# A projection whose gates run ahead of its products, on one core: order, sums and mixing moved

## The chip, the cores and the metric

One Trainium2 chip, one of its cores. The metric is the device time of one execution of the whole program in microseconds (us). TensorE (PE) multiplies matrices into PSUM banks; VectorE (DVE), ScalarE (ACT) and GpSimd (POOL) work on tiles of 128 partitions in SBUF; transfers are issued by the queue of SyncE (SP) and by ACT. Each engine runs its own instructions strictly in the order in which they stand, and waits for the others by semaphores.

## The reference, cut to what matters

Two layers. The first (gMLP and dilated attention) is left out here, since nothing in it changes. The second is RWKV-7 time mixing. Its part that matters:

```python
xx = concatenate([zeros_like(h[:, :1]), h[:, :-1]], axis=1) - h
xr, xw, xk, xv, xa, xg = [h + xx * mu[i] for i in range(6)]
r = xr @ w_r
k = xk @ w_k
v = xv @ w_v
g = xg @ w_g
logw = -softplus(-(w0 + tanh(xw @ w1) @ w2)) - 0.5
decay = exp(-exp(logw))
a = sigmoid(a0 + (xa @ a1) @ a2)
kk = hs(k * k_k)
kk = kk * rsqrt(maximum(sum(kk * kk, axis=-1, keepdims=True), 1e-24))
k = k * (1.0 + (a - 1.0) * k_a)
...                                   # rwkv7_scan over r, decay, k, v, kk, a, then the group norm of y
bonus = sum(rh * kh * r_k, axis=-1, keepdims=True) * vh
y = (y + bonus) * silu(g)
return y @ w_o
```

Sequence 1024, width 1024, 16 heads of 64, all float32. Every product of the projections is made of three passes (high by high, high by low, low by high), with each operand split into a rounded part and a rest: `hi` by ACT, `lo = raw - hi` by DVE or POOL.

## The kernel before, in words

The second layer works in this order: the low-rank first factors (`lora`), then three projections r, k and v of four column blocks of 256 (`CB`) each. The list `plan` has the twelve blocks, j = 0 to 3 for r, 4 to 7 for k, 8 to 11 for v. The projections' inputs are mixtures of a token and the one before it: `mixed` makes, for one half `f` of the sequence (512 tokens), eight tiles: `xm` (ACT L736 a scaling, DVE L737 the rest), `xh` (ACT L739) and `xl` (L740, by DVE for odd and by POOL for even tiles). The tiles of r's half f are given back by r's last block only, so k's mixing of half 0 follows r's last product of half 0, and that of half 1 follows r's last product of all; v's mixing stands to k in the same way. After v come the gate's product and the scan over chunks. The gate's mixing of half 1 goes through DRAM (`mixed_out`, L750 to L755): eight units, each with three tiles `xm`, `xh`, `xl` of the ring `s2`, which has seven places, and two stores. Block j = `XD` issues it. The ring `s2` also serves `xm` of `mixed` and `rt`, the tile by which r and v are written out of PSUM (L842, L855).

For r and k a piece is 128 channels (index p) by 512 tokens (half f): 24 matmuls into one of three banks `bA`. There are 16 pieces, and a block of columns has four. In k, `Prep.__call__` takes each finished piece: `ks` is its copy (L789); `pz` holds the gates' two products (two matmuls each, second low-rank factors `rw_w2` and `rw_a2`, loaded and split per piece by `second`, L778 and L779); `tanh` follows (L797); DVE runs a sum along the tokens of each chunk of 64 (L799, L802); ACT exponentiates it both ways (L803, L804); then DVE and POOL build the operands `AR` (L809, L811, L812) and `BK` (L813, L814, L817) of the scan, and `tz` for the bonus (L815, L816 on POOL, L820). Two sums over the channels of each head are made by matmuls with `sel` (L822 of the squares of `ks`, L823 of `tz`), 32 columns of which two are used, into a bank of their own per piece, copied out by L825 and stored. `AR` and `BK` are stored in DRAM (`A_d`, `BK_d`) for the scan.

Up to the scan, the order of the instructions on each engine is chosen when the program is built, by a scheduler of the framework; from the scan on it is written out by hand in tables that the change does not touch.

Of the kernel before, what the change touches and what calls it, by code (L numbers as in the profile page):

```python
# [757 lines left out]
class Prep:  # L758


    def __init__(self, g, a, pool):
# [4 lines left out]

    def second(self, p):

        if p not in self.w2:
# [1 line left out]
            self.w2 = {p: []}
            for n in ("rw_w2", "rw_a2"):
                raw = self.pool.tile([P, P], F32, name="w2", bufs=1)
                for i in range(2):
                    nc.sync.dma_start(raw[64 * i:64 * i + 64], self.a[n][0][:, p * P:(p + 1) * P])
                hi = self.pool.tile([P, P], F32R, name=n + "h", bufs=2)
                lo = self.pool.tile([P, P], F32R, name=n + "l", bufs=2)
                nc.scalar.activation(hi, raw, AF.Copy)  # L778
                nc.vector.tensor_tensor(lo, raw, hi.bitcast(F32), OP.subtract)  # L779
                self.w2[p].append((hi, lo))  # L780
        return self.w2[p]

    def __call__(self, p, f, pk):
        g, nc, pool = self.g, self.g.nc, self.pool
        sl = slice(f * 512, (f + 1) * 512)
# [4 lines left out]
        rt = pool.tile([P, 512], F32, name="rl", bufs=2)  # L790
        nc.sync.dma_start(rt, g.r_d[p][:, sl])
        pz = g.bB([P, 2, 512], "pz")
        tz = pool.tile([P, 2, 512], F32, name="tz", bufs=2)
        for i, ((wh, wl), src, b) in enumerate(zip(self.second(p), (self.TH, self.UA), (g.w0h, g.a0h))):
            nc.tensor.matmul(pz[:, i], wh, src[:, sl], start=True, stop=False)
            nc.tensor.matmul(pz[:, i], wl, src[:, sl], start=False, stop=True)
            nc.scalar.activation(tz[:, i], pz[:, i], AF.Tanh, bias=b[:, p:p + 1], scale=0.5)  # L797
# [1 line left out]
        nc.vector.tensor_scalar(tw, tw, 0.5, 0.5, op0=OP.mult, op1=OP.add)  # L799
# [742 lines left out]
```

## Time and profile before

| | |
|---|---|
| time, median of three runs (lowest, highest) | 1494.33 us (1488.99, 1495.18) |
| the profiled execution: its time, its span | 1504.67 us, 1502.9 us |
| mean granted clock of TensorE | 0.943 |
| busy share of the span: PE, DVE, ACT, POOL | 89%, 62%, 43%, 38% |
| mean transfer rate | 142 GB/s |

The profiled execution took 10.3 us more than the median of the runs, so a sum over its trace is first made in its own times and then set against the median. In the trace, times are from the start of the span; r's products run from 625 to 728 us, those of k from 728 to some 892 us, the last sums of k's pieces at 947 us, and v's last piece is written out at 1005 us.

### The profile page before, as it was taken

The page shows a single profiled execution, that of the slowest core. Times are in us where ns is not written, and L with a number is a line of the kernel's source. Part 1 is how long each engine was busy: PE and PEld are TensorE (multiplying, and loading weights), DVE is VectorE, ACT ScalarE, POOL GpSimd, SP SyncE. Part 2 cuts the span into 40 slices and gives each one's busy share as a digit, 9 for nine tenths or more (in the row PEclk, how much of TensorE's full clock was granted, in tenths as well). Part 3 has the DMA queues.
Part 4 walks back from the last instruction along what each step waited for, and adds up shares of the span by engine and source line. Part 5 has one row for each costly group of instructions (what it writes and reads, how often), then busy time and mean ns, then how long its engine had stood idle before and what let it go on. Part 6 is the DMA issues. An engine that isn't in the chain of part 4 may idle for free.

```text
span 1502.9 us, 28032 instructions
## 1 busy us (share of the span) xinstructions
PE 1330.6 (89%) x11237; PEld 1130.5 (75%) x11237; DVE 933.2 (62%) x1504; ACT 645.2 (43%) x1236; POOL 565.1 (38%) x381
## 2 busy tenths in 40 slices
PE   5899999799989999999998779998878888978877
PEld 5887788688887799878754447996667777768777
DVE  8752536653565337650897898134577778777884
ACT  4422535543553234552654654134444444453322
POOL 9750102130114412211542543024654444477751
PEclk9999999899999999999998989999988999978998
DMA  6386436340523434142385557338486666765412
GB/s 217 85 273 174 126 117 165 80 131 8 168 78 115 139 127 139 36 150 78 88 250 145 121 150 187 78 98 237 110 256 171 163 158 163 204 207 197 153 31 98
DMA packets 256083, 213.19 MB, mean 142 GB/s; under 512 B 80416, under 2 KB 216192, under 8 KB 255952
## 3 DMA queue, kind: packets, MB, share of 16 engines
q1 hardware_dynamic: 232576, 196.11, 45.1%
q10 hardware_dynamic: 23376, 15.27, 3.8%
q8 instruction: 89, 1.46, 0.4%
q14 instruction: 42, 0.34, 0.1%
HBM read 139.90 MB, written 71.43 MB: 141 GB/s over the span
## 4 chain that ended last, share of the span: by engine, by line
PE 50%; DVE 19%; DMA 10%; ACT 7%; issue 7%; POOL 4%; SPq 3%; ACTq 0%; DVEq 0%; POOLq 0%
PE pj L153 33%; DVE tm L1140 2%; PE pt L572 2%; PE pj L1454 2%; PE pj L711 1%; PE pj L942 1%; DMA Nt<-MA 1%; DMA sg_d<-XT 1%; PE py L1274 1%; PE op L580 1%; ACT wh L105 1%; ACT xm L736 1%; DVE xm L737 1%; PE sp L559 1%; PE sp L562 1%
## 5 line engine op out<-in xcount | busy, mean ns | idle before, releaser
L106 POOL TENSOR_TENSOR wl<-wraw,wh 128x1024 fp32r<-128x1024 f32 x38 | 93.7, 2467 | 164.1 <-ACT wh L105 152.3
L106 DVE TENSOR_TENSOR wl<-wraw,wh 128x1024 fp32r<-128x1024 f32 x46 | 72.2, 1574 | 101.2 <-ACT wh L105 53.4
L153 PE MATMUL pj<-hh,wh 128*128 128x512 f32 x320 | 127.3, 398 | 0.0
L153 PE MATMUL pj<-hh,wl 128*128 128x512 f32 x320 | 126.6, 396 | 0.0
L153 PE MATMUL pj<-hl,wh 128*128 128x512 f32 x320 | 126.6, 396 | 0.0
L105 ACT ACTIVATE wh<-wraw 128x1024 fp32r<-128x1024 f32 x84 | 88.1, 1055 | 67.4 <-DMA wraw<-in_w_in_even_dram 23.0
L153 PE MATMUL pj<-xh,wh 128*128 128x512 f32 x256 | 103.4, 406 | 2.5 <-ACT ks L789 2.4
L153 PE MATMUL pj<-xl,wh 128*128 128x512 f32 x256 | 103.1, 403 | 2.6 <-DVE xl L740 2.6
L153 PE MATMUL pj<-xh,wl 128*128 128x512 f32 x256 | 102.7, 401 | 0.3 <-POOL wl L106 0.3
L566 DVE CUSTOM_DVE_ANT_0 sc<-sp,tb 128x128 f32<-128x128 f32 (+3 forms) x64 | 48.2, 754 | 56.7 <-PE sp L562 48.7
L1454 PE MATMUL pj<-wh,yh 128*128 128x256 f32 x256 | 76.0, 297 | 5.6 <-DVE x L1458 4.1
L1454 PE MATMUL pj<-wh,yl 128*128 128x256 f32 x256 | 75.0, 293 | 4.5 <-POOL yl L106 4.5
L737 DVE SCALAR_TENSOR_TENSOR xm<-hT,pr,xm 128x512 f32<-128x512 f32 x56 | 50.0, 935 | 45.2 <-ACT xm L736 44.8
L153 PE MATMUL pj<-wh,hh 128*128 128x256 f32 x256 | 74.8, 295 | 2.8 <-ACT hh L265 2.5
L153 PE MATMUL pj<-wh,hl 128*128 128x256 f32 x256 | 75.1, 294 | 1.2 <-DVE hl L266 1.2
L153 PE MATMUL pj<-wh,yl 128*128 128x256 f32 x256 | 73.7, 288 | 1.9 <-POOL yl L624 1.9
L1454 PE MATMUL pj<-wl,yh 128*128 128x256 f32 x256 | 74.6, 291 | 0.0
L153 PE MATMUL pj<-wl,hh 128*128 128x256 f32 x256 | 74.3, 291 | 0.0
L153 PE MATMUL pj<-wh,yh 128*128 128x256 f32 x256 | 73.2, 286 | 1.1 <-ACT yh L623 1.1
L153 PE MATMUL pj<-wl,yh 128*128 128x256 f32 x256 | 72.8, 284 | 0.0
L153 PE MATMUL pj<-wh,xh 128*128 128x256 f32 x256 | 72.2, 282 | 0.2
L153 PE MATMUL pj<-wl,xh 128*128 128x256 f32 x256 | 72.2, 282 | 0.0
(323 smaller groups left out, 4131.2 us busy)
## 6 DMA issues: line engine op xcount, KB each, us to landing
wraw<-in_w_in_even_dram SPq DMA_DIRECT2D x28, 512.0 KB
tb<-tb SPq DMA_DIRECT2D x16, 512.0 KB
A_d<-AR SPq DMA_DIRECT2D x16, 512.0 KB
wraw<-in_rw_wg_dram SPq DMA_DIRECT2D x16, 512.0 KB
BK<-BK_d SPq DMA_DIRECT2D x16, 512.0 KB
A<-A_d SPq DMA_DIRECT2D x30, 256.0 KB
xt<-in_x_dram SPq DMA_DIRECT2D x8, 512.0 KB
dv<-vt SPq DMA_DIRECT2D x16, 256.0 KB
```

What stands on the lines that cost most here:

```text
L105: nc.scalar.activation(hi, raw, AF.Copy)
L106: sub.tensor_tensor(lo, raw, hi.bitcast(F32), OP.subtract)
L153: nc.tensor.matmul(ps, a(k), b(k), start=(n == 0), stop=(n == 3 * KT - 1))
L559: nc.tensor.matmul(sp[:, c0:c1], qs[:, b * P:(b + 1) * P], kh[:, c0:c1], start=True, stop=False)
L562: nc.tensor.matmul(sp[:, c0:c1], qs[:, b * P:(b + 1) * P], kl[:, c0:c1], start=False, stop=True)
L566: nc.vector.tensor_tensor_reduce(sc[:, :n], sp[:, :n], tb[:, off:off + n], 1.0, BIG, OP.add, OP.min, mn)
L572: nc.tensor.transpose(pt[:, j - j0, :], sc[:, j * P:(j + 1) * P], g.ident)
L580: nc.tensor.matmul(op[:, s0:QW], vt[:, j, :], pth[j // 4][:, j % 4, s0:QW], start=(j == 0), stop=False)
L711: nc.tensor.matmul(ps, x[:, 2 * kk + i, :], y[:, i, o:o + 512], start=(n == 0), stop=(n == 47))
L737: nc.vector.scalar_tensor_tensor(t, hT[kk, f][:, j, 0:512], g.pr[:, i, k:k + 1], t, op0=OP.mult, op1=OP.add)
L1140: nc.vector.tensor_tensor(tv, D[:, :, 0:t, 0:t], Nd[:, :, t, 0:t][:, :, None, :].to_broadcast([P, 4, t, t]), OP.mult)
L1454: nc.tensor.matmul(ps[:, i, :], u[:, k], v[:, k % 4], start=(k == 0 and j == 0), stop=(k == KT - 1 and j == 2))
```

## The change

`Prep.__call__` is split in three. `gates(p, f)` does what does not need the product (load of r's piece, the gates' products, tanh, the running sum, both exponentials, and two new affine steps on ACT, L822 and L824 of the new code, that take over the scaling of the gate from DVE). `operands` does what needs it: POOL now makes `ks` times the inverse decay (L834) into the place of `BK`'s second half, and DVE multiplies this into both halves (L837, L838); the decays `E` have a column of ones ahead of each chunk, so that `AR` is one instruction (L835) instead of two. `sum` makes the sums of the piece before, with the columns of `sel` moved by p, so that all pieces of a half add up in one bank, which is copied out and stored once per half (L862). `project` calls them: for each piece the gates, then the 24 matmuls, then the sum of the piece before. `second` loads and splits the second factors per block of four pieces and takes the raw tile from the ring `s2`. While j is 4 to 7, the order on PE is that of the program text. `XD` is 8, so `mixed_out` is issued in v's first block.

```diff
-XD = 6
+XD = 8
...
-    g.sel = c.tile([P, 32], F32, name="sel")
+    g.sel = c.tile([P, 40], F32, name="sel")
     nc.vector.memset(g.sel, 0.0)
-    nc.vector.memset(g.sel[0:64, 0:1], 1.0)
-    nc.vector.memset(g.sel[64:128, 1:2], 1.0)
+    nc.vector.memset(g.sel[0:64, 7:8], 1.0)
+    nc.vector.memset(g.sel[64:128, 15:16], 1.0)
...
         self.UA = pool.tile([P, S], F32R, name="UA")
...
+        self.E = [pool.tile([P, 8, CH + 1], F32, name=f"E{i}") for i in range(2)]
+        for E in self.E:
+            g.nc.vector.memset(E[:, :, 0:1], 1.0)
+        self.w2, self.sums, self.n = {}, {}, 0
+        self.due = None
+
+    def second(self, c):
+
+        if c not in self.w2 and c < D // CB:
             g, nc = self.g, self.g.nc
...
+            raw = g.s2([P, 2, CB], F32, "w2")
+            for i in range(2):
+                for j, n in enumerate(("rw_w2", "rw_a2")):
+                    nc.sync.dma_start(raw[64 * i:64 * i + 64, j], self.a[n][0][:, c * CB:(c + 1) * CB])
+            hi = self.pool.tile([P, 2, CB], F32R, name="w2h", bufs=2)
+            lo = self.pool.tile([P, 2, CB], F32R, name="w2l", bufs=2)
+            nc.scalar.activation(hi, raw, AF.Copy)
+            nc.vector.tensor_tensor(lo, raw, hi.bitcast(F32), OP.subtract)
+            self.w2[c] = hi, lo
+
+    def project(self, x, w, c, fs=(0, 1)):
+        g = self.g
+        wh, wl = w
+        self.second(c)
+        for f in fs:
+            for m in range(2):
+                t = self.gates(2 * c + m, f)
+                ps = g.bA([P, 512], "pj")
+                mm3(g.nc, ps, lambda k: wh(k, m), lambda k: wl(k, m),
+                    lambda k: x[0][k // 2, f][:, k % 2, 0:512], lambda k: x[1][k // 2, f][:, k % 2, 0:512])
+                self.sum()
+                self.operands(2 * c + m, f, ps, *t)
+            if f == 0:
+                self.second(c + 1)
+
+    def gates(self, p, f):
+
         g, nc, pool = self.g, self.g.nc, self.pool
-        sl = slice(f * 512, (f + 1) * 512)
+        sl, o = slice(f * 512, (f + 1) * 512), slice((p % 2) * P, (p % 2 + 1) * P)
+        wh, wl = self.w2[p // 2]
+        rt = pool.tile([P, 512], F32, name="rl", bufs=2)
+        nc.sync.dma_start(rt, g.r_d[p][:, sl])
+        pz = g.bB([P, 2, 512], "pz")
+        tz = pool.tile([P, 2, 512], F32, name="tz", bufs=2)
+        for i, (src, b) in enumerate(((self.TH, g.w0h), (self.UA, g.a0h))):
+            nc.tensor.matmul(pz[:, i], wh[:, i, o], src[:, sl], start=True, stop=False)
+            nc.tensor.matmul(pz[:, i], wl[:, i, o], src[:, sl], start=False, stop=True)
+            nc.scalar.activation(tz[:, i], pz[:, i], AF.Tanh, bias=b[:, p:p + 1], scale=0.5)
+        tw, ta = tz[:, 0], tz[:, 1]
+        nc.vector.tensor_scalar(tw, tw, 0.5, 0.5, op0=OP.mult, op1=OP.add)
+        nc.vector.tensor_tensor_scan(tw, g.smask.rearrange("p c t -> p (c t)"), tw, 0.0, op0=OP.mult, op1=OP.add)
+        E, self.n = self.E[self.n % 2], self.n + 1
+        nc.scalar.activation(E[:, :, 1:CH + 1], tw.rearrange("p (c t) -> p c t", t=CH), AF.Exp, scale=-C0)
+        nc.scalar.activation(tw, tw, AF.Exp, scale=C0)
+        nc.gpsimd.tensor_copy(g.EC[:, p, f * 8:(f + 1) * 8, None], E[:, :, CH:CH + 1])
+        BK = pool.tile([P, 8, 2, CH], F32, name="BK", bufs=2)
+        nc.scalar.activation(BK[:, :, 0, :], ta.rearrange("p (c t) -> p c t", t=CH), AF.Identity,
+                             bias=g.kkn[:, p:p + 1], scale=g.kkn[:, p:p + 1])
+        nc.scalar.activation(ta, ta, AF.Identity, bias=g.kam[:, p:p + 1], scale=g.kah[:, p:p + 1])
+        return rt, tw, ta, E, BK
+
+    def operands(self, p, f, pk, rt, En, ta, E, BK):
+        g, nc, pool = self.g, self.g.nc, self.pool
         kk, rk = g.pr[:, 8, p:p + 1], g.pr[:, 10, p:p + 1]
         c3 = lambda t: t.rearrange("p (c t) -> p c t", t=CH)
         ks = pool.tile([P, 512], F32, name="ks", bufs=2)
         nc.scalar.activation(ks, pk, AF.Copy)
...
         AR = pool.tile([P, 8, 2, CH], F32, name="AR", bufs=2)
...
+        nc.gpsimd.tensor_tensor(BK[:, :, 1, :], c3(ks), c3(En), OP.mult)
+        nc.vector.scalar_tensor_tensor(AR[:, :, 0, :], c3(ks), kk, E[:, :, 0:CH], op0=OP.mult, op1=OP.mult)
+        (nc.vector if p % 2 else nc.gpsimd).tensor_tensor(AR[:, :, 1, :], c3(rt), E[:, :, 1:CH + 1], OP.mult)
+        nc.vector.tensor_tensor(BK[:, :, 0, :], BK[:, :, 0, :], BK[:, :, 1, :], OP.mult)
+        nc.vector.tensor_tensor(BK[:, :, 1, :], c3(ta), BK[:, :, 1, :], OP.mult)
         nc.gpsimd.tensor_tensor(ta, ta, ks, OP.mult)
-        nc.vector.tensor_tensor(BK[:, :, 1, :], c3(ta), En, OP.mult)
-        sq = ks
-        nc.scalar.activation(sq, ks, AF.Square, scale=kk)
         nc.vector.scalar_tensor_tensor(ta, rt, rk, ta, op0=OP.mult, op1=OP.mult)
...
+        nc.scalar.activation(ks, ks, AF.Square, scale=kk)
+        self.due = p, f, ks, ta
         nc.sync.dma_start(g.A_d[:, f * 8:(f + 1) * 8, p], AR)
         nc.sync.dma_start(g.BK_d[0:64, f * 8:(f + 1) * 8, p], BK[0:64])
         for j in range(2):
             nc.sync.dma_start(g.BK_d[64:128, f * 8:(f + 1) * 8, p, 1 - j], BK[64:128, :, j])
+
+    def sum(self):
+
+        if self.due is None:
+            return
+        g, nc = self.g, self.g.nc
+        (p, f, sq, ta), self.due = self.due, None
+        if p == 0:
+            self.sums[f] = g.bC([64, 512], "pt")
+        ps = self.sums[f]
+        nc.tensor.matmul(ps[0:32], g.sel[:, 7 - p:39 - p], sq, start=p == 0, stop=p == KT - 1)
+        nc.tensor.matmul(ps[32:64], g.sel[:, 7 - p:39 - p], ta, start=p == 0, stop=p == KT - 1)
+        if p == KT - 1:
+            sl = slice(f * 512, (f + 1) * 512)
+            so = g.s2([64, 512], F32, "xm")
+            nc.vector.tensor_copy(so, ps)
+            nc.sync.dma_start(g.ss_d.rearrange("e q s -> (e q) s")[:, sl], so[0:16])
+            nc.sync.dma_start(g.bo_d.rearrange("e q s -> (e q) s")[:, sl], so[32:48])
...
-    def ev_k(c):
-        return lambda m, f, ps: prep(2 * c + m, f, ps)
+    def keys(g, x, w, c, fs=(0, 1)):
+        prep.project(x, w, c, fs)
...
-    for i, n, fn, ld, ev in ((0, "rw_wr", chan_major, load_wm, ev_r), (2, "rw_wk", chan_major, load_wm, ev_k),
+    for i, n, fn, ld, ev in ((0, "rw_wr", chan_major, load_wm, ev_r), (2, "rw_wk", keys, load_wm, lambda c: c),
                              (3, "rw_wv", token_major, load_wk, ev_v)):
...
+    order = ExitStack()
     for j, (i, W, fn, ld, ev, c) in enumerate(plan):
+        if j == 4:
+            order.enter_context(tc.manual_schedule(engines={mybir.EngineType.PE}))
+        if j == 8:
+            prep.sum()
+            order.close()
```

What that does to the order of the instructions, at three places. On PE, at the end of r: `pj_6775` before and `pj_6779` after are r's last piece, `pj_6863` and `pj_6896` k's first, `pz_6880` the gates of k's first piece. Before:

```order
L153 MATMUL pj_6775<-xh_6247,wh_6515 128x512
L153 MATMUL pj_6775<-xl_6248,wh_6515 128x512
L153 MATMUL pj_6775<-xh_6247,wl_6516 128x512
L153 MATMUL pj_6863<-xh_6699,wh_6635 128x512
L153 MATMUL pj_6863<-xl_6700,wh_6635 128x512
L153 MATMUL pj_6863<-xh_6699,wl_6636 128x512
```

and now:

```order
L153 MATMUL pj_6779<-xl_6252,wh_6519 128x512
L153 MATMUL pj_6779<-xh_6251,wl_6520 128x512
L811 MATMUL pz_6880<-TH_6007,w2h_6874 128x512
L812 MATMUL pz_6880<-TH_6007,w2l_6875 128x512
L811 MATMUL pz_6880<-UA_6008,w2h_6874 128x512
L812 MATMUL pz_6880<-UA_6008,w2l_6875 128x512
L153 MATMUL pj_6896<-xh_6703,wh_6639 128x512
L153 MATMUL pj_6896<-xl_6704,wh_6639 128x512
```

The gates of k's first piece now stand between r's last and k's first matmul; before, the gates of the first two pieces stood among the products of r's first five pieces.

On DVE, at the same place. The rows L737 and L740 of tiles on `hT_4790` and `hT_4791` are the end of k's mixing of half 1, and L809 to L815 before are the first pieces' operands. Before:

```order
L740 TENSOR_TENSOR xl_6804<-xm_6810,xh_6803 128x512
L740 TENSOR_TENSOR xl_6816<-xm_6822,xh_6815 128x512
L737 SCALAR_TENSOR_TENSOR xm_6841<-hT_4791,pr_4802,xm_6841 128x512
L809 SCALAR_TENSOR_TENSOR AR_6920<-ks_6888,pr_4802,tz_6893 128x8x63
L811 TENSOR_SCALAR AR_6920<-ks_6888,pr_4802 128x8
L813 SCALAR_TENSOR_TENSOR BK_6921<-tz_6893,ks_6888 128x8x64
L812 TENSOR_TENSOR AR_7000<-rl_6970,tz_6973 128x8x64
L740 TENSOR_TENSOR xl_6828<-xm_6834,xh_6827 128x512
```

and now:

```order
L740 TENSOR_TENSOR xl_6808<-xm_6814,xh_6807 128x512
L740 TENSOR_TENSOR xl_6820<-xm_6826,xh_6819 128x512
L737 SCALAR_TENSOR_TENSOR xm_6845<-hT_4791,pr_4802,xm_6845 128x512
L740 TENSOR_TENSOR xl_6832<-xm_6838,xh_6831 128x512
L737 SCALAR_TENSOR_TENSOR xm_6850<-hT_4791,pr_4802,xm_6850 128x512
L740 TENSOR_TENSOR xl_6844<-xm_6850,xh_6843 128x512
L783 TENSOR_TENSOR w2l_6875<-w2_6869,w2h_6874 128x512
L815 TENSOR_SCALAR tz_6881<-tz_6881 128x512
L816 SCALAR_TENSOR_TENSOR tz_6881<-smask_4820,tz_6881 128x512
```

The split of the second factors (L783), which the gates on PE read, stands behind the whole of k's mixing; before, those of the first pieces stood ahead of r's mixing of half 1.

On ACT, at the end of k. L855 before and L888 after write v's pieces out of PSUM, L750 and L752 are `mixed_out`. Before, `mixed_out` had ended a hundred rows ahead of v's first piece:

```order
L804 ACTIVATE L_7983<-L_7983 128x512
L797 ACTIVATE tz_7961<-pz_7960,a0h_4806 128x512
L105 ACTIVATE wh_8579<-wraw_8575 128x1024
L105 ACTIVATE wh_8583<-wraw_8577 128x1024
L778 ACTIVATE rw_w2h_8045<-w2_8042 128x128
L855 ACTIVATE rt_8408<-pj_8359 128x256 x2
```

and now:

```order
L105 ACTIVATE wh_8316<-wraw_8310 128x1024
L750 ACTIVATE xm_8065<-hT_4790,onemu_4814 128x512
L752 ACTIVATE xh_8066<-xm_8065 128x512
L750 ACTIVATE xm_8074<-hT_4791,onemu_4814 128x512
L752 ACTIVATE xh_8075<-xm_8074 128x512
L750 ACTIVATE xm_8083<-hT_4791,onemu_4814 128x512
L752 ACTIVATE xh_8084<-xm_8083 128x512
L888 ACTIVATE rt_8141<-pj_8092 128x256 x2
L888 ACTIVATE rt_8195<-pj_8146 128x256 x2
L888 ACTIVATE rt_8249<-pj_8200 128x256 x2
```

All eight units of `mixed_out`, and two splits of v's weights among them, now stand ahead of the first row that frees a bank of v, and they stand behind the last square of k's last piece.

More of the change, by code (lines that the diff above doesn't have):

```diff
@@ L764, in __init__ @@
         self.UA = pool.tile([P, S], F32R, name="UA")
-        self.w2 = {}
-    def second(self, p):
-        if p not in self.w2:
-            g, nc = self.g, self.g.nc
[L771 to L781, printed above, removed]
@@ L789, in __call__ @@
         nc.scalar.activation(ks, pk, AF.Copy)
[L790 to L797, printed above, removed]
@@ L798, in __call__ @@
-        tw, ta = tz[:, 0], tz[:, 1]
-        nc.vector.tensor_scalar(tw, tw, 0.5, 0.5, op0=OP.mult, op1=OP.add)
-        L = pool.tile([P, 512], F32, name="L", bufs=2)
-        E = tw
-        nc.vector.tensor_tensor_scan(L, g.smask.rearrange("p c t -> p (c t)"), tw, 0.0, op0=OP.mult, op1=OP.add)
-        nc.scalar.activation(E, L, AF.Exp, scale=-C0)
-        nc.scalar.activation(L, L, AF.Exp, scale=C0)
-        E3, En = c3(E), c3(L)
-        nc.gpsimd.tensor_copy(g.EC[:, p, f * 8:(f + 1) * 8, None], E3[:, :, CH - 1:CH])
@@ L814, in __call__ @@
-        nc.vector.scalar_tensor_tensor(BK[:, :, 0, :], BK[:, :, 0, :], g.kkn[:, p:p + 1], En, op0=OP.mult, op1=OP.mult)
-        nc.vector.tensor_scalar(ta, ta, g.kah[:, p:p + 1], g.kam[:, p:p + 1], op0=OP.mult, op1=OP.add)
+        AR = pool.tile([P, 8, 2, CH], F32, name="AR", bufs=2)
+        nc.gpsimd.tensor_tensor(BK[:, :, 1, :], c3(ks), c3(En), OP.mult)
+        nc.vector.scalar_tensor_tensor(AR[:, :, 0, :], c3(ks), kk, E[:, :, 0:CH], op0=OP.mult, op1=OP.mult)
+        (nc.vector if p % 2 else nc.gpsimd).tensor_tensor(AR[:, :, 1, :], c3(rt), E[:, :, 1:CH + 1], OP.mult)
@@ L816, in __call__ @@
+        nc.vector.tensor_tensor(BK[:, :, 0, :], BK[:, :, 0, :], BK[:, :, 1, :], OP.mult)
+        nc.vector.tensor_tensor(BK[:, :, 1, :], c3(ta), BK[:, :, 1, :], OP.mult)
         nc.gpsimd.tensor_tensor(ta, ta, ks, OP.mult)
-        nc.vector.tensor_tensor(BK[:, :, 1, :], c3(ta), En, OP.mult)
-        sq = ks
-        nc.scalar.activation(sq, ks, AF.Square, scale=kk)
         nc.vector.scalar_tensor_tensor(ta, rt, rk, ta, op0=OP.mult, op1=OP.mult)
-        pss = g.bC([64, 512], "pt")
-        nc.tensor.matmul(pss[0:32], g.sel, sq, start=True, stop=True)
@@ L823, in __call__ @@
-        nc.tensor.matmul(pss[32:64], g.sel, ta, start=True, stop=True)
-        so = pool.tile([64, 512], F32, name="so", bufs=1)
-        nc.vector.tensor_copy(so, pss)
-        nc.sync.dma_start(g.ss_d[:, p, sl], so[0:2])
-        nc.sync.dma_start(g.bo_d[:, p, sl], so[32:34])
+        nc.scalar.activation(ks, ks, AF.Square, scale=kk)
+        self.due = p, f, ks, ta
         nc.sync.dma_start(g.A_d[:, f * 8:(f + 1) * 8, p], AR)
```

7 lines of the change are left out of this document (removed).

## The prediction

> **What bounds it now.** First the page's chain, then a table of four stretches: r's products (to 728), k's mixing of half 1 (to 743), the pieces of k (to 948), the rest of v (to 1006).
>
> ```profile
> PE 50%; DVE 19%; DMA 10%; ACT 7%; issue 7%; POOL 4%; SPq 3%; ACTq 0%; DVEq 0%; POOLq 0%
> 626.00:728.00 102.00, 101.75 (x439) 81.95 (x438) 42.08 (x52) 45.50 (x74) 21.66 (x13) 1.00 0.28 89
> 728.00:743.00 15.00, 15.00 (x66) 12.15 (x65) 14.03 (x16) 11.37 (x20) 7.82 (x5) 1.00 0.21 62
> 743.00:948.00 205.00, 173.14 (x734) 112.46 (x733) 171.83 (x229) 104.27 (x184) 85.49 (x56) 0.92 0.66 175
> 948.00:1006.00 58.00, 58.00 (x484) 57.57 (x483) 14.99 (x15) 17.67 (x38) 8.18 (x8) 1.00 0.18 50
> ```
>
> Columns after the length: busy time of PE, PEld, DVE, ACT, POOL, then clock, DMA share, GB/s. PE is full in three stretches; in the third it idles 32 of 205 us at a mean clock of 0.92, while DVE is busy 172 and POOL 85. These two do not run side by side, as the timeline shows:
>
> ```profile
> 739.64 0.68 DVE L813 SCALAR_TENSOR_TENSOR BK<-tz,ks 128x512 f32<-128x512 f32 x1
> 739.68 1.80 POOL L740 TENSOR_TENSOR xl<-xm,xh 128x512 fp32r<-128x512 f32 x1 [1.30 <-ACT xh L739]
> 740.25 1.78 DVE L812 TENSOR_TENSOR AR<-rl,tz 128x512 f32<-128x512 f32 x1
> 741.95 0.68 DVE L740 TENSOR_TENSOR xl<-xm,xh 128x512 fp32r<-128x512 f32 x1
> 747.16 2.62 POOL L106 TENSOR_TENSOR wl<-wraw,wh 128x1024 fp32r<-128x1024 f32 x1 [0.92 <-ACT wh L105]
> 747.44 2.88 DVE L740 TENSOR_TENSOR xl<-xm,xh 128x512 fp32r<-128x512 f32 x1
> ```
>
> POOL's subtraction ends at 741.48, and DVE's L812, begun at 740.25, ends 0.55 later, at 742.03: 1.78 us where half of its kind take 0.69. So POOL's 512 elements cost DVE 1.1 us, its 1024 elements 2.88 - 0.69 = 2.2 us. DVE and POOL are one resource here, "the pair", and the third stretch is the pair's.
>
> The Trainium skill, "SBUF — State Buffer", section "Who interferes with whom", has the rule: a DVE instruction with two SBUF inputs and a GpSimd instruction that reads SBUF exclude each other through a shared port pair, for a whole instruction. These rows agree, and the rule speaks against this change, which hands work from DVE to POOL.
>
> **The pair's work in a piece.** Durations (least, median, largest, ns) by tile:
>
> ```profile
> L799 DVE TENSOR_SCALAR tz<-tz x16: 394/422/2185, 650.2 to 935.0; 128x512 f32<-128x512 f32 x16
> L802 DVE TENSOR_TENSOR_SCAN L<-smask,tz x16: 1205/1218/2204, 652.5 to 935.4; 128x512 f32<-128x512 f32 x16
> L809 DVE SCALAR_TENSOR_TENSOR AR<-ks,pr,tz x16: 711/738/1783, 738.9 to 937.9; 128x504 f32<-128x504 f32 x16
> L811 DVE TENSOR_SCALAR AR<-ks,pr x16: 215/230/1271, 739.5 to 926.7; 128x8 f32<-128x8 f32 x16
> L813 DVE SCALAR_TENSOR_TENSOR BK<-tz,ks x16: 656/680/1343, 739.6 to 939.2; 128x512 f32<-128x512 f32 x16
> L815 DVE TENSOR_SCALAR tz<-tz,kah,kam x16: 529/538/2661, 743.9 to 940.6; 128x512 f32<-128x512 f32 x16
> L816 POOL TENSOR_TENSOR tz<-tz,ks x16: 1257/1659/2484, 744.5 to 941.3; 128x512 f32<-128x512 f32 x16
> L817 DVE TENSOR_TENSOR BK<-tz,L x16: 666/686/1761, 750.2 to 942.6; 128x512 f32<-128x512 f32 x16
> L820 DVE SCALAR_TENSOR_TENSOR tz<-rl,pr,tz x16: 737/752/2832, 753.3 to 943.3; 128x512 f32<-128x512 f32 x16
> L812 DVE TENSOR_TENSOR AR<-rl,tz x8: 677/685/1794, 740.2 to 938.6; 128x512 f32<-128x512 f32 x8
> L825 DVE COPY so<-pt x16: 672/682/683, 759.7 to 947.8; 64x512 f32<-64x512 f32 x16
> L779 DVE TENSOR_TENSOR rw_w2l<-w,rw_w2h x16: 256/286/2505, 625.4 to 928.0; 128x128 fp32r<-128x128 f32 x16
> L106 POOL TENSOR_TENSOR wl<-wraw,wh x7: 2345/2556/2922, 747.2 to 929.6; 128x1024 fp32r<-128x1024 f32 x7
> L106 DVE TENSOR_TENSOR wl<-wraw,wh x7: 1194/1212/1225, 755.0 to 932.5; 128x1024 fp32r<-128x1024 f32 x7
> ```
>
> On DVE an instruction starts some 0.07 us before the last one's recorded end (L813 at 739.64, L812 at 740.25: 0.61 for 0.68), so each counts 0.07 less.
>
> - Before: L799 0.42, L802 1.22, L809 0.74, L811 0.23, L813 0.68, L814 as L809 0.74, L815 0.54, L817 0.69, L820 0.75, L825 0.68, half an L812 0.34, two L779 0.57: 7.6, less 12.5 times 0.07, is 6.7. POOL: L816 1.1 and half an L812 0.55. Together 8.35 us.
> - After: the first two 1.64, `AR` in one 0.74, half its second part 0.34, two plain products for `BK` 1.38, the bonus 0.75, a quarter of a wide split 0.17: 5.0, less 0.47, is 4.55. POOL has L816's twin, the new product with `ks`, and half an `AR`: 2.75. Together 7.3 us. The new POOL product has no row; its ends are nothing (if it never met DVE) and 1.66 (L816's own median), and I take 1.1, what a POOL product of this size took from DVE above.
>
> So 2.15 us of DVE go and 1.1 of POOL come: 1.05 us per piece, 17 over k. The affine steps moved to ACT (two of some 0.7 us) hide: ACT is busy 104 of 205 us. Thirty-two small stores become four; nothing in the chain waits for them, so I count nothing, and if that cover were gone a store would cost SP one issue.
>
> **The stretch in sum.** Before, from 743: 16 times 8.35, less 5 us that the first two pieces had done ahead; seven pairs of weight splits (1.14 + 2.2 each, 23.4); v's mixing, 16 xm at 0.68, 8 + 8 xl at 0.62 and 1.1 (24.6); `mixed_out` (12.3): 189 of 205 us, 92%. After, from k's first gates to the last bonus: 117 + 1.2 (two copies) + five pairs of splits, 16.7 (two fall into v) + 24.6, and no `mixed_out`: 159.5.
>
> **When k starts.** PE's first instruction after r is now a gate that waits for the split L783, queued on DVE behind k's whole mixing of half 1.
>
> ```profile
> 728.57 0.58 ACT L842 ACTIVATE rt<-pj 128x512 f32<-128x512 f32 x1
> 734.84 2.38 DVE L740 TENSOR_TENSOR xl<-xm,xh 128x512 fp32r<-128x512 f32 x2
> 737.14 1.78 DVE L737 SCALAR_TENSOR_TENSOR xm<-hT,pr,xm 128x512 f32<-128x512 f32 x1
> 755.64 1.04 PE L823 MATMUL pt<-tz,sel 128*32 128x512 f32 x2
> 756.61 0.50 PE L153 MATMUL pj<-xh,wh 128*128 128x512 f32 x1
> 660.81 55.48 PE pj L153 x238
> 947.77 39.67 PE pj L153 x336
> ```
>
> r ends at 728, by the first row. Eight gate matmuls leave r (55.48 / 238 = 0.233 each): 1.9 us earlier. The mixing is at 738.9 after the third row; an xl, an xm, a wait for POOL and the last xl follow (0.6 + 0.7 + 1.1 + 0.6), then the split 0.6: 742.5, less 1.9, is 740.7. The raw factors wait for a place in `s2` that the first xl frees (736.6, less 1.9), land some 4 us later and do not end last. So PE idles 15 us where it made 64 of k's matmuls. That by itself costs the pair nothing: its own queue is full until then.
>
> **When k ends.** PE needs for a piece 28 x 0.233 = 6.5 and for a sum 2 x 0.97 (755.64 to 756.61): 8.45 us; the pair 7.3, with splits 8.1. If PE set the pace: 740.7 + 16 x 6.5 + 14 x 1.94 = 872 for the last product, and 23 for the bonus behind it (7.3, v's second mixing 12.3, a pair of splits 3.3): 895. If the pair did, at 92% as now: 740.7 + 159.5 / 0.92 = 914. Both nearly tie, and each sum waits for a chain through ACT, POOL and DVE, so I take 910.
>
> **What v then waits for.** ACT frees v's first bank only behind all of `mixed_out`, which follows the last square and bonus. PE can fill three banks meanwhile, then stands.
>
> ```profile
> L751 DVE SCALAR_TENSOR_TENSOR xm<-hT,pr,xm x8: 733/746/752, 744.3 to 783.3; 128x512 f32<-128x512 f32 x8
> L750 ACT ACTIVATE xm<-hT,onemu x8: 705/710/726, 737.6 to 782.5; 128x512 f32<-128x512 f32 x8
> L750 ACT ACTIVATE xm<-hT,onemu x5: 705/710/726, 767.4 to 782.5; 128x512 f32<-128x512 f32 x5
> L752 ACT ACTIVATE xh<-xm x8: 613/630/634, 747.0 to 784.6; 128x512 fp32r<-128x512 f32 x8
> L105 ACT ACTIVATE wh<-wraw 128x1024 fp32r<-128x1024 f32 x84 | 88.1, 1055 | 67.4 <-DMA wraw<-in_w_in_even_dram 23.0
> 863.77 1.92 PE L822 MATMUL pt<-ks,sel 128*32 128x512 f32 x2 [3.63 <-ACT ks L819]
> 1005.19 0.64 ACT L855 ACTIVATE rt<-pj 128x256 f32<-128x256 f32 x2
> ```
>
> From 910: the last sum and its copy ahead of the first unit on DVE 2.7; eight units that take turns on ACT, DVE, ACT (0.71 + 0.75 + 0.63 + 0.1 for handing over), 17.6; two splits 2.1; the first evacuation 0.7: PE goes on at 933. Then 624 of v's 768 matmuls at 39.67 / 336 = 0.118 are 73.7, and a slow clock after the wait 1.7 (a pair of sums takes 1.92 after a gap of 3.63, not 1.04; the table has clock 1.00 where PE is full). The last evacuation ends at 1009.2, against 1005.8 by the last row: +3.4 us. What follows v is the same text and starts from that evacuation. In the profiled execution's terms 1504.7 + 3.4 = 1508.1; against the runs' median 1494.3 + 3.4 = 1497.7, and I predict 1498.
>
> **Rivals.** (1) Faster: the pair stops binding. For it: 7.3 us of pair against PE's 8.45; against: the splits and v's mixing, and that the saved DVE time goes to POOL. With k ending at 895, v's last evacuation comes at 1009.2 - 15 - 1.7 = 992.5, 13 us earlier: 1481. It decides if waits of PE for a sum stay under a microsecond each. (2) Slower: `mixed_out` paced by its stores. The ring has seven places and a unit takes three, so the fourth unit waits for the first unit's store. Before, the last five units began between 767.4 and 782.5 (the row of five), 3.8 us apart, among other work; at that pace eight take 7 x 3.8 + 2.1 = 28.7, not 17.6: +11, and with the pair at its 92% (914) +4: 1494.3 + 3.4 + 15 = 1513. It decides from 2.8 us a unit, where the sum passes +7.5. (3) Slower by the clock: waits of PE over some 2.5 us halve its clock for 3.4 us, 1.7 us each; six such waits in k, +10: 1508. The Trainium skill, "TensorE: Matmul & The Clock Gate", section "What's actually happening", gives half rate after an idle window of about 3.4 us; by that rule only longer waits count, and the rival falls. The trace has 1.92 after 3.63, which does not tell the two apart.
>
> **How the numbers follow.** A measurement here tells 0.5%, 7.5 us, from no change. Forecast (within that): 0.45. Rival 1: 0.20. Rivals 2 and 3: 0.25 and 0.10. The range takes rival 1's 1481 plus 2 and reaches past rival 2 to both slow rivals in part: 1483 to 1517.
>
> **What would show it.** PE idle some 15 us after r's last product; DVE's busy time per piece lower but POOL's higher, the two still filling k's stretch; the last `tz` for a bonus near 910; then ACT's eight units back to back, a second wait of PE of 10 to 20 us, and v ending near 1009. The prediction is wrong if DVE has wide gaps in k, or if v's first evacuation comes soon after its product.

## The result: 1.1% slower, where 0.2% was forecast

The changed kernel took 1509.38 us (median of four runs, 1507.08 to 1512.36) against 1494.25 for the kernel before, a ratio of 1.011 with a 95% interval of 1.008 to 1.0139. That is 15 us. It lies inside the predicted range, but 11 us above the predicted 1498 and near the slow rival 2 (1513). The profiled execution took 1512.36 us, its span was 1510.6.

The lines of the profile that answer to those of before. The chain, by engine:

```profile
PE 52%; DVE 17%; DMA 10%; ACT 8%; issue 6%; POOL 4%; SPq 3%; ACTq 0%; DVEq 0%; POOLq 0%
```

Four stretches of the trace, counted from the end of r's last evacuation (720.3; it was 729.2 in the trace of before): k's mixing; first gates to last bonus; up to TensorE's restart in v; the rest of v. Columns as in the prediction's table.

```profile
720.30:733.20 12.90, 0.00 (x0) 0.00 (x0) 11.61 (x13) 9.88 (x17) 6.64 (x4) 0.56 0.18 56
733.20:908.90 175.70, 145.32 (x604) 99.67 (x604) 137.70 (x138) 112.71 (x175) 102.42 (x69) 0.96 0.54 149
908.90:932.70 23.80, 6.91 (x52) 5.87 (x52) 13.23 (x15) 12.40 (x21) 7.45 (x5) 0.73 0.67 230
932.70:1011.00 78.30, 78.28 (x635) 77.83 (x636) 16.64 (x16) 22.71 (x50) 10.55 (x8) 0.97 0.29 84
```

In the second stretch DVE has 138 and POOL 102 of 176 us, and in 159.6 of them one or both are busy (worked out from all their rows): 91%, where before had 92% (198.7 of 214.9 us from r's last evacuation to its last bonus). TensorE is what differs. Its waits from r's end to v's end, in the view of waits (who, for what, us in total, times, longest), first of the changed kernel, then the largest of before:

```profile
PE pj L153 <- ACT rt L888: 16.9, 1, 16.9
PE pt L857 <- ACT ks L841: 15.4, 8, 3.0
PE pz L811 <- ACT tz L813: 14.9, 16, 2.4
PE pz L811 <- ACT w2h L782: 14.7, 1, 14.7
```

```profile
PE pt L822 <- ACT ks L819: 10.8, 6, 3.6
PE pt L823 <- DVE tz L820: 9.5, 4, 3.7
PE pz L795 <- ACT tz L797: 4.6, 2, 4.2
```

Four causes hold 62 us of idle TensorE after, where all of before's make 32. Each is a place: v's first bank, the sums, the tanh between a piece's two gate products, and k's start. The half clock cost 7 us after and 14.5 before, and the matmuls themselves 7 us less after (all three worked out from the rows of TensorE and its clock; the first of the four waits begins 1.8 us ahead of r's last evacuation, so that the table below has 60 of the 62 us).

**k's start.** ACT, DVE and PE, from the timeline:

```profile
732.59 0.63 ACT L782 ACTIVATE w2h<-w 128x512 fp32r<-128x512 f32 x1 [0.70 <-DMA w<-in_rw_a_dram]
733.25 0.69 DVE L783 TENSOR_TENSOR w2l<-w,w2h 128x512 fp32r<-128x512 f32 x1 [0.35 <-ACT w2h L782]
733.27 0.80 PE L811 MATMUL pz<-TH,w2h 128*128 128x512 f32 x1 [14.75 <-ACT w2h L782]
737.17 0.79 PE L811 MATMUL pz<-UA,w2h 128*128 128x512 f32 x1 [2.38 <-ACT tz L813]
```

The 15 us are there as forecast, though the transfer of the raw factors ended last, by 0.35 us.

**A piece.** Two pieces of k on PE. At the end of the first its sums wait for nothing (a light piece, as they are called below), at the end of the second they do:

```profile
762.54 0.62 PE L857 MATMUL pt<-ks,sel 128*32 128x512 f32 x1
762.54 0.62 PE L858 MATMUL pt<-tz,sel 128*32 128x512 f32 x1
763.52 0.50 PE L811 MATMUL pz<-TH,w2h 128*128 128x512 f32 x1
765.03 0.50 PE L811 MATMUL pz<-UA,w2h 128*128 128x512 f32 x1 [0.78 <-ACT tz L813]
773.62 1.04 PE L857 MATMUL pt<-ks,sel 128*32 128x512 f32 x2 [2.30 <-ACT ks L841]
```

The second gate product waits some 0.8 us for the tanh of the first, in every piece but the first, where it is 2.38. The three longer waits of the sums in k's first three blocks (up to 773.62, 811.29 and 849.63) are each for a piece whose product had just ended when a weight split began on POOL (at 763.55, 801.22 and 838.89), and those at the end of k follow v's mixing; that these set the waits is read from the times and was not tried.

**`mixed_out`.** ACT behind k's last square, first and last unit:

```profile
908.16 0.72 ACT L841 ACTIVATE ks<-ks,pr 128x512 f32<-128x512 f32 x1 [6.88 <-POOL tz L839]
908.79 0.71 ACT L750 ACTIVATE xm<-hT,onemu 128x512 f32<-128x512 f32 x1
911.43 0.63 ACT L752 ACTIVATE xh<-xm 128x512 fp32r<-128x512 f32 x1 [1.94 <-DVE xm L751]
...
931.49 0.63 ACT L752 ACTIVATE xh<-xm 128x512 fp32r<-128x512 f32 x1 [1.31 <-DVE xm L751]
932.03 1.74 ACT L888 ACTIVATE rt<-pj 128x256 f32<-128x256 f32 x6
```

Eight units and two splits of weights take 23.2 us, then three banks are freed at once.

### The profile page after: what moved, and what is told of

The parts are those of the page before. It is cut to its first block, busy times and chain, and to the rows that moved or that the text cites. A ratio compares the mean times of both kernels' runs of the same rounds, so it can differ in the third digit from the quotient of the medians.

```text
span 1510.6 us, 27893 instructions
## 1 busy us (share of the span) xinstructions
PE 1308.5 (87%) x11237; PEld 1124.2 (74%) x11237; DVE 900.3 (60%) x1416; ACT 664.1 (44%) x1240; POOL 590.7 (39%) x397
## 4 chain that ended last, share of the span: by engine, by line
PE 52%; DVE 17%; DMA 10%; ACT 8%; issue 6%; POOL 4%; SPq 3%; ACTq 0%; DVEq 0%; POOLq 0%
PE pj L153 33%; PE pj L981 3%; PE pj L1493 2%; PE pt L572 2%; PE pj L711 1%; DVE tm L1179 1%; DMA kl<-dk 1%; PE py L1313 1%; PE pm L1087 1%; PE sp L559 1%; DVE rt L198 1%; PE sp L562 1%; ACT wh L105 1%; DVE AR L835 1%; DVE xl L740 1%
## 5 line engine op out<-in xcount | busy, mean ns | idle before, releaser
L106 POOL TENSOR_TENSOR wl<-wraw,wh 128x1024 fp32r<-128x1024 f32 x38 | 92.8, 2443 | 194.5 <-ACT wh L105 181.5
L153 PE MATMUL pj<-wh,xh 128*128 128x256 f32 x256 | 73.9, 289 | 16.9 <-ACT rt L888 16.9
L737 DVE SCALAR_TENSOR_TENSOR xm<-hT,pr,xm 128x512 f32<-128x512 f32 x56 | 49.6, 924 | 45.8 <-ACT xm L736 45.4
L1493 PE MATMUL pj<-wl,yh 128*128 128x256 f32 x256 | 76.0, 297 | 0.0
L153 PE MATMUL pj<-wh,xl 128*128 128x256 f32 x256 | 73.4, 287 | 0.0
```

What stands on the lines that cost most here:

```text
L106: sub.tensor_tensor(lo, raw, hi.bitcast(F32), OP.subtract)
L153: nc.tensor.matmul(ps, a(k), b(k), start=(n == 0), stop=(n == 3 * KT - 1))
L737: nc.vector.scalar_tensor_tensor(t, hT[kk, f][:, j, 0:512], g.pr[:, i, k:k + 1], t, op0=OP.mult, op1=OP.add)
L1493: nc.tensor.matmul(ps[:, i, :], u[:, k], v[:, k % 4], start=(k == 0 and j == 0), stop=(k == KT - 1 and j == 2))
```

## The experiments

Two theories at first. **Places**: TensorE's waits carry the loss, so each that is taken away comes back. **Pair**: DVE and POOL, which exclude one another, set k's length, so that only what shortens their work or their idle time counts. Times of a trace are given from the end of r's last evacuation ("from r"), since the part ahead of r varies by some 8 us between executions. "Pair busy" is the time in which DVE or POOL is busy up to the last bonus; "lost" is TensorE's idle time and what the half clock took, from r's last evacuation to v's last. Each ratio is to runs of before on the same chip.

| kernel | ratio to before (95%) | last bonus, from r | v's end, from r | pair busy | PE lost: idle + half clock |
|---|---|---|---|---|---|
| before, two traces | 1 | 214.9, 215.3 | 276.7, 277.1 | 198.7, 198.8 | 31.9 + 14.5, 33.5 + 13.8 |
| changed | 1.0110 (1.0080 to 1.0139) | 188.6 | 290.7 | 172.1 | 60.2 + 7.1 |
| e1 mixing later | 1.0066 (1.0031 to 1.0100) | 189.2 | 284.8 | 171.2 | 49.2 + 14.7 |
| e2 mixing in k | 1.0078 (1.0047 to 1.0108) | 201.1 | 283.9 | 182.8 | 47.9 + 14.3 |
| e3 factors early | 1.0085 (1.0052 to 1.0119) | 182.3 | 284.3 | 168.1 | 51.5 + 12.7 |
| e4 tanh behind | 1.0140 (1.0108 to 1.0172) | 190.7 | 292.3 | 173.5 | 55.7 + 14.5 |
| e5 mixing in parts, early | 0.9936 (0.9909 to 0.9962) | 181.6 | 266.2 | 167.0 | 33.0 + 14.6 |
| e6 sums two behind, tanh | 0.9998 (0.9977 to 1.0020) | 167.6 | 275.1 | 164.2 | 45.3 + 9.5 |
| e7 ks on DVE | 1.0071 (1.0047 to 1.0095) | 181.7 | 285.7 | 163.2 | 54.5 + 9.3 |
| e9 e5 and e6 | 0.9849 (0.9823 to 0.9875) | 161.8 | 245.0 | 159.4 | 18.0 + 5.2 |
| e10 with ks on DVE | 0.9790 (0.9761 to 0.9820) | 155.7 | 237.8 | 154.4 | 15.3 + 4.7 |
| e11 all products on DVE | 0.9757 (0.9730 to 0.9784) | 147.5 | 231.7 | 143.3 | 10.2 + 3.4 |
| e12 before, mixing in parts | 0.9904 (0.9876 to 0.9931) | 195.3 | 260.9 | 184.6 | 25.6 + 6.1 |

**e1: the mixing one block later.**

```diff
-XD = 8
+XD = 9
```

> The changed kernel with the gate's mixing issued one block later, in v's second block instead of its first; nothing else differs. Changed kernel 1509, before 1494. Theory of places (TensorE's waits at fixed places carry the loss): the 16.9 us wait for v's first bank and the 2.1 us of slow clock behind it go, v's last evacuation comes 19 us earlier, 1490 us (1487 to 1494). Theory of the pair (VectorE and GpSimd together set k's length): the same here, since the mixing lies behind k in both. Rival: the mixing, now between v's evacuations, holds up the later banks or the gate's loads, and less than half is won: 1500 or more.

1504.95 us against 1497.3 for before in the same runs: the rival's side. The first bank is free at once, but after four pairs of evacuations the same eight units stand in a row again. The groups of evacuations and units, and PE's wait:

```profile
L888 ACT ACTIVATE rt<-pj x32: 363/379/393, 914.8 to 1010.1; 128x256 f32<-128x256 f32 x32
L750 ACT ACTIVATE xm<-hT,onemu x8: 706/709/727, 930.4 to 951.7; 128x512 f32<-128x512 f32 x8
PE pj L153 <- ACT rt L888: 8.8, 1, 8.8
```

The wait fell from 16.9 to 8.8 us and v's end by 5.9. TensorE idled 11 us less, but the half clock took 7.6 more (14.7 against 7.1). The units need to be apart, not only later, as e5 shows. By their ratios alone e1 and the changed kernel are not told apart; the wait in the trace is what tells them apart.

**e2: the mixing in k.**

```diff
-XD = 8
+XD = 6
```

> The changed kernel with the gate's mixing back in k's third block, where the kernel before has it. Theory of places: the wait for v's first bank goes as in the run before this one, and k, paced by TensorE, takes the mixing's 12 us of VectorE and GpSimd into its slack: 1490 to 1493 us. Theory of the pair: VectorE and GpSimd were busy 124 of 137 us in k's middle, 12 more leave them 1 us of slack, and k ends some 10 us later: 1500 us (1497 to 1504).

The last bonus came 12.5 us later, as much as the mixing's work for the pair (12.3), although the pair had 17 us of idle time there:

```profile
L840 DVE SCALAR_TENSOR_TENSOR tz<-rl,pr,tz x16: 720/741/1814, 764.4 to 927.8; 128x512 f32<-128x512 f32 x16
```

That is as the theory of the pair has it. The time, 1510.19 us, is above both expectations, and its ratio is not told apart from e1's or the changed kernel's; v's ends of e1 and e2 are alike in the traces too (283.9 and 284.8).

**e3: the first factors early.**

```diff
     lora(g, hT, wt, prep.TH, prep.UA)
+    prep.second(0)
```

> The changed kernel with the first second-factor tile loaded and split right after the low-rank first factors, ahead of r's mixing of half 1, so that k's first gates wait for nothing behind r. Theory of places: the 14.75 us wait of TensorE between r and k goes, and the slow clock at k's start with it: 1509 - 16 = 1493 us. Theory of the pair: the operands of k's first pieces still wait for VectorE to finish k's mixing, TensorE runs three pieces ahead and then stands, and the last bonus comes 0 to 4 us earlier: 1505 to 1509 us.

1509.89 us, 1 us past the pair's range and far from the 1493 of the places (before took 1497.3 in these runs, 3 us more than at first). 6.4 us of v's end came back, between the theories and nearer the pair's. The 14.7 us are gone from the view of waits; the sums took 4.2 us of them:

```profile
PE pt L857 <- ACT ks L841: 19.6, 8, 3.2
PE pj L153 <- ACT rt L888: 16.8, 1, 16.8
PE pz L811 <- ACT tz L813: 14.9, 15, 3.2
```

The half clock took 5.6 more (12.7 against 7.1). From r, the first bonus starts 15 us earlier than in the changed kernel, the fourth 6.4, and the lead stays there. By their ratios e3 and the changed kernel are not told apart; by the traces the 6 us are there.

**e4: both tanh behind the gates.**

```diff
             nc.tensor.matmul(pz[:, i], wl[:, i, o], src[:, sl], start=False, stop=True)
-            nc.scalar.activation(tz[:, i], pz[:, i], AF.Tanh, bias=b[:, p:p + 1], scale=0.5)
+        for i, b in enumerate((g.w0h, g.a0h)):
+            nc.scalar.activation(tz[:, i], pz[:, i], AF.Tanh, bias=b[:, p:p + 1], scale=0.5)
```

> The changed kernel with all four matmuls of a piece's gates written ahead of both tanh, instead of a tanh between the two pairs. In the trace of the changed kernel the second pair stands 0.78 us behind the first tanh in each of 16 pieces, 12.5 us. Theory of places: all of it comes back, 1509 - 12 = 1497 us. Theory of the pair: with 0.78 us less a piece would take 7.94 us of TensorE against some 7.7 of VectorE and GpSimd, so the waits for the sums take most of it: 1503 to 1508 us.

Neither: 1519.98 us, ratio 1.0140, not faster at all. The waits for the tanh are gone, those for sums and for v's bank grew:

```profile
PE pj L153 <- ACT rt L889: 22.7, 1, 22.7
PE pt L858 <- ACT ks L842: 17.9, 6, 4.2
PE pz L811 <- ACT w2h L782: 14.8, 1, 14.8
```

The last bonus came at 190.7, 2 us later. From the end of its product to the end of its bonus a piece takes 7.1 to 13.8 us here but for the last (20.6), while TensorE is through with the next product, and at the sum, 7.6 us later in the light pieces. So a third theory, of the **chain**: with a sum one product behind, TensorE, DVE and POOL wait for each other by turns, and neither is full.

**e5: the mixing in parts, and e3's edit.**

```diff
-def mixed_out(g, hT, i, f, dst):
+def mixed_out(g, hT, i, f, dst, ks):
...
-    for k in range(KT):
+    for k in ks:
...
+    prep.second(0)
...
-        if j == XD:
-            mixed_out(g, hT, 5, 1, g.xg_d)
+        if j >= XD:
+            mixed_out(g, hT, 5, 1, g.xg_d, (range(0), range(0, 2), range(2, 5), range(5, 8))[j - XD])
```

> The changed kernel with two edits: the gate's mixing is issued in parts, two units in v's second block, three in its third and three in its fourth, so that no more than three stand between two evacuations of v; and the first second-factor tile is loaded and split early, as in the third run. Changed kernel 1509, before 1495. Theory: k's length is set by the work of each piece between product and bonus, and the loss against before is v's late start. The third run won 5.5 us at k's start; the wait for v's first bank (16.8 us there) and the slow clock behind it (2 us) should go, and nothing replace it, since three units take 8 us and TensorE has three banks ahead: 1509 - 5 - 18 = 1486 us (1482 to 1491), faster than before. Rival: the units' loads on VectorE, the ring's places and the stores hold up v's evacuations again, as in the first run, where 8.8 us of the 16.9 came back in v's middle: 1495 to 1503.

1488.23 us, ratio 0.9936, as the theory expected. The evacuations begin with the last square, the units spread over 49 us of v, and no wait of PE for a bank is left. Against e3, which has the other of the two edits, v's end comes 18.1 us earlier:

```profile
L888 ACT ACTIVATE rt<-pj x32: 361/378/386, 906.0 to 990.3; 128x256 f32<-128x256 f32 x32
L750 ACT ACTIVATE xm<-hT,onemu x8: 707/716/725, 921.8 to 970.6; 128x512 f32<-128x512 f32 x8
```

**e6: the sums two products behind.** With e4's edit, and the ring at six places to make room:

```diff
-N2 = 7
+N2 = 6
...
-        tz = pool.tile([P, 2, 512], F32, name="tz", bufs=2)
+        tz = pool.tile([P, 512], F32, name="tw", bufs=2), pool.tile([P, 512], F32, name="ta", bufs=3)
...
-        self.due = p, f, ks, ta
+        self.due.append((p, f, ks, ta))
...
+    def sum(self, lag=2):
+        if len(self.due) < lag:
+            return
```

> The changed kernel with the tanh behind all four gate matmuls, as in the fourth run, and each piece's two sums made two products later instead of one (the tile that ends as the bonus gets a third buffer; the ring s2 has six places instead of seven to make room). Theory of the chain: in the fourth run TensorE stood at sums, because a piece takes 7 to 13 us from product to bonus and the next product only 5.6 to 6.5; two products of cover hide that, a piece takes TensorE's 7.9 us, and k's last bonus comes 12 to 18 us earlier than in the changed kernel: 1492 to 1498 us. Theory of the pair: VectorE and GpSimd together are busy 160 of the 176 us from k's first gates to its last bonus, the cover only lets them fill the rest, and TensorE then waits for the banks that ScalarE and the pair free: 4 to 8 us earlier, 1501 to 1506 us.

1495.76 us, ratio 0.9998: the theory of the chain gave 1492 to 1498. Its reason was half of it: the last bonus came 21 us earlier (167.6; 12 to 18 were expected), and it is now the pair that stops it there, busy 164.2 of 167.6 us, 98%. The window from r to the last bonus, and the waits:

```profile
727.00:894.60 167.60, 142.88 (x600) 99.76 (x600) 148.80 (x147) 118.58 (x186) 96.08 (x72) 0.93 0.60 161
```

```profile
PE pj L153 <- ACT rt L889: 20.5, 1, 20.5
PE pz L811 <- ACT w2h L782: 13.2, 1, 13.2
PE pt L858 <- ACT ks L842: 9.4, 5, 3.2
```

So the 91% of the changed kernel was no ceiling of the pair; the coupling through the sums kept it there. The tanh alone gained nothing (e4); the second product of cover without the tanh edit, and the third buffer that it needs without the cover, were not tried.

**e7: the new product on DVE.**

```diff
-        nc.gpsimd.tensor_tensor(BK[:, :, 1, :], c3(ks), c3(En), OP.mult)
+        nc.vector.tensor_tensor(BK[:, :, 1, :], c3(ks), c3(En), OP.mult)
```

> The changed kernel with the product of ks and the inverse decay on VectorE instead of GpSimd. Theory of the pair (a GpSimd operation of 512 elements keeps VectorE off for 1.1 us, a VectorE one takes 0.62): 16 x 0.5 = 8 us less work for the pair and a shorter chain: 1501 to 1505 us. Rival, GpSimd runs beside VectorE and costs it little: VectorE gets 16 x 0.62 = 10 us more, 1509 to 1519 us.

1506.24 us, 1 us past the pair's range, away from the rival (before took 1496.55 in these runs, 2 us more than at first). By the ratios alone it is not told apart from the changed kernel; the trace carries the reading. The pair's work fell by 8.9 us (172.1 to 163.2), 0.56 per piece, and the last bonus by 6.9: a product costs less on the busier engine. The window from r to the last bonus has DVE at 140.8 although it got 16 operations more (149.3 in the changed kernel), since it no longer waits inside others:

```profile
727.90:909.60 181.70, 143.55 (x605) 98.64 (x606) 140.79 (x167) 123.17 (x191) 83.92 (x57) 0.93 0.55 149
```

**e8: the kernel before, again.**

> The kernel before, unchanged, for a second trace: the first one's execution took 10 us more than the median of the runs. If the 10 us lie ahead of r, as a comparison of the first trace with those of the changed kernels suggests, the time from r's last evacuation to v's last is 277 us as in the first trace, to within 2.

277.1 against 276.7, as expected; the last bonuses are 0.4 us apart. The last bonus and v's evacuations of this trace:

```profile
L820 DVE SCALAR_TENSOR_TENSOR tz<-rl,pr,tz x16: 736/752/1779, 751.1 to 941.6; 128x512 f32<-128x512 f32 x16
L855 ACT ACTIVATE rt<-pj x32: 362/378/387, 903.4 to 1003.7; 128x256 f32<-128x256 f32 x32
```

v's evacuations start 38 us ahead of k's last bonus: before let k's tail run beside v's products. In the changed kernel the first of them starts 23 us behind it.

**e9: e5 and e6 together.**

> The changed kernel with the edits of the fifth run (mixing in parts, factors early) and of the sixth (tanh behind the gates, sums two products behind, six places in the ring). In the sixth run VectorE and GpSimd were busy 164 of the 168 us from r's end to the last bonus, and TensorE still stood 12 us for the first gates and 20.5 us for v's first bank. Theory of the pair: the last bonus comes at most 4 us earlier than there (164 us after r's end), but the wait for v's bank goes, and of the wait at k's start what TensorE can use ahead; v's last evacuation 250 to 255 us after r's end instead of 275: 1496 - 22 = 1474 us (1468 to 1480). Rival: v's evacuations now fall into k's last pieces and ScalarE's order holds them, or the six places hold up the mixing: 1483 to 1492.

1472.77 us against 1495.5, as the theory expected; v's end, at 245.0, was 5 us earlier than that, and the last bonus came 5.8 us earlier than in e6, where at most 4 were expected. **e10** adds e7's edit, **e11** moves the products of L839 and L836 as well:

```diff
-        nc.gpsimd.tensor_tensor(ta, ta, ks, OP.mult)
+        nc.vector.tensor_tensor(ta, ta, ks, OP.mult)
...
-        (nc.vector if p % 2 else nc.gpsimd).tensor_tensor(AR[:, :, 1, :], c3(rt), E[:, :, 1:CH + 1], OP.mult)
+        nc.vector.tensor_tensor(AR[:, :, 1, :], c3(rt), E[:, :, 1:CH + 1], OP.mult)
```

> The run before this one with the product of ks on VectorE, as in the seventh run. Theory of the pair: now that VectorE and GpSimd are full through k, the 0.5 us per piece that the seventh run moved should show in k's length, 8 us, the last bonus 8 us earlier, and the time 4 to 8 us less than the run before this one. Rival: TensorE sets the pace by then (222 us of matmuls from r's end to v's end): 0 to 2 us less.

> As the run before this one, with every 512-element product of k's pieces on VectorE (the product of ta and ks in each piece and AR's second part in every other besides): GpSimd keeps only the weights' and mixtures' rests. Theory of the pair: another 24 operations at 0.5 us, 12 us less for the pair; where TensorE does not bind, up to 8 us less time than the run before this one, else none. Rival: VectorE alone then has 160 of 160 us and its queue delays what ScalarE and TensorE wait for: 3 to 8 us more.

1463.77 and 1459.48 us, so 9.0 us less than e9 (4 to 8 expected) and 4.3 less than e10. The last bonus moved by 6.1 and 8.2 us, v's end by 7.2 and 6.1; the pair's work by 5.0 (0.31 per operation) and 11.1 (24 operations, 0.46 each). The windows from r to the last bonus of e9, e10 and e11, one of each:

```profile
728.70:890.50 161.80, 143.85 (x591) 95.78 (x589) 147.50 (x144) 113.26 (x180) 100.91 (x70) 0.96 0.61 165
```

```profile
732.30:888.00 155.70, 140.36 (x601) 97.47 (x600) 138.64 (x162) 113.98 (x181) 79.16 (x55) 0.97 0.64 173
```

```profile
733.70:881.20 147.50, 137.26 (x596) 95.86 (x594) 139.68 (x185) 112.85 (x180) 43.38 (x32) 0.99 0.68 183
```

From e9 to e11 POOL loses 57 us and DVE, with 41 operations more, 8. In e11 PE and DVE are both nearly full. By their intervals e10 is faster than e9; e11 and e10 overlap.

**e12: before, with the mixing in parts** (e5's edit of `mixed_out` in the kernel before; its first lines as there):

```diff
-XD = 6
+XD = 8
...
-        if j == XD:
-            mixed_out(g, hT, 5, 1, g.xg_d)
+        if j >= XD:
+            mixed_out(g, hT, 5, 1, g.xg_d, (range(0), range(0, 2), range(2, 5), range(5, 8))[j - XD])
```

> The kernel before with one edit: the gate's mixing taken out of k and issued in parts in v's second to fourth block, as in the fifth run. Theory of the pair: k loses 12.3 us of VectorE and GpSimd, its last bonus comes some 12 us earlier and v's end 8 to 12 us: 1484 to 1488 us, as fast as the fifth run, so that the new order of a piece by itself is worth nothing there. Rival: TensorE's waits in k come from single pieces' chains and not from the sum of the work, and v's end moves 0 to 4 us: 1492 to 1496.

1481.33 us, faster than forecast: the pair lost 14.1 us up to the last bonus, that came 19.6 earlier and v's end 15.8. The rival is out.

```profile
L820 DVE SCALAR_TENSOR_TENSOR tz<-rl,pr,tz x16: 725/751/2912, 755.5 to 923.3; 128x512 f32<-128x512 f32 x16
L855 ACT ACTIVATE rt<-pj x32: 364/378/389, 889.8 to 989.3; 128x256 f32<-128x256 f32 x32
```

With the mixing placed well, the old order of a piece (0.9904) is not slower than the new one (e5, 0.9936; the intervals overlap). With the mixing in k as before has it, the new order is slower (e2, 1.0078). It showed a gain only with two products of cover for the sums (e9, with the early factors and the tanh behind as well); the old one with such cover was not tried.

## Why the prediction was right and wrong

Its steps, from r's end (in the prediction's own times r's end of the changed kernel is 729.2 - 1.9 = 727.3):

| step | predicted | measured | error so far |
|---|---|---|---|
| first gates | 740.7: +13.4 | +13.0 | -0.4 |
| last bonus | 910: +182.7 | +188.6 | +5.9 |
| PE goes on in v | 933: +205.7 | +212.4 | +6.7 |
| v's last evacuation | 1009.2: +281.9 | +290.7 | +8.8 |

Against before's trace, v's end was to come 3.4 us later and came 290.7 - 276.7 - 1.9 = 12.1 us later. Behind it the changed kernel took 499.6 us to its end, before 497.0 and 494.6: the 3 to 5 us that are left of the 15. All fourteen traces spread from 490.4 to 501.5 there, in an order that has nothing plain to do with the edits; what sets it stays open.

- **Right: the pair's work.** From the first gates to the last bonus it was predicted at 159.5 us and was 159.6, with the price of a POOL product taken as 1.1 us. So close an agreement is in part luck: the same reckoning gave 189 us for the pieces of k before, where its rows have 185.2. The moves to DVE in e7, e10 and e11 measured 0.31 to 0.56 us gained per operation, against 1.1 - 0.62 = 0.48.
- **Right: the two places.** TensorE's 15 us at k's start and its wait for v's first bank (16.9 us, forecast 10 to 20). e5 showed the second by removing it.
- **Wrong: "I take 910", in "When k ends".** This is the step that failed, and half of the miss. The pair's own reckoning gave 914, and 2 us more were measured; the compromise with 895 was the error. Its reason, that each sum waits for a chain through ACT, POOL and DVE, adds time to either bound and so speaks for an end behind 914, not ahead of it. That the pair would again be 92% busy was carried over from before without a reason: it came near (91%), but e6, at 98%, shows that the sums one product behind set it, so the size was right by luck. The 8.45 us for PE came near the 8.7 of a light piece (gates begin at 783.8, 792.5 and 801.2) only by two errors against each other: the two sums take 0.98 us together and not 1.94, and the gates' four matmuls 2.08 (763.52 to 765.60) and not 0.93, 0.78 of it the wait for the tanh. Missing too were 15.4 us for the sums.
- **Mis-sized: `mixed_out`.** A unit took 2.65 us ((23.2 - 2.1) / 8), not 2.2: no more than +0.8 in the end, since the first unit starts on ACT (908.79) beside the last sum and its copy, for which 2.7 us had been set ahead of it. That is short of rival 2's 2.8.
- **Mis-sized: the rest of v**, 78.3 us instead of 76.2. In this trace the clock is at half up to 4.2 us behind the restart, which costs 2.1 and not 1.7. The last evacuation stands on ACT behind a step of the next mixing that waits 2.17 us for DVE, and ends 2.4 us after the slot of v's last matmul (1008.63 to 1011.01; 2.3 in the trace of before), where the sum leaves 0.8.
- **The rivals.** Rival 2 was nearest in its sum, but not in its reason: its first part, the pair at 92% (+4), came in full (+5.9), its second (+11 for the units) hardly (+0.8). Rival 1 needed waits for a sum under a microsecond; eight were up to 3.0. Rival 3 went the other way: the half clock took 7.1 us instead of 14.5 (the last section has what sets it in these traces).
- **Not asked:** what before had that would be lost. There v's evacuations start 38 us ahead of k's last bonus (e8), and in the trace of before TensorE has only two waits, 1.5 us in all, from v's first matmul (897.45) to v's end:

```profile
PE pz L796 <- DVE rw_w2l L779: 1.0, 1, 1.0
PE pz L795 <- ACT rw_w2h L778: 0.5, 1, 0.5
```

So a late end of k cost TensorE next to nothing there. In e5 and e9, with the mixing in parts, v's evacuations start with the last bonus or just behind it (181.5 and 181.6; 164.3 and 161.8).
